# Seven products of block sums for two of eight pairs of k tiles in w_up and w_down, w_up as [token, column], operands at another remainder modulo 128

## The chip, the cores and the metric

One Trainium2 chip, of which the kernel uses 1 core in one launch. The metric is the device time of that launch in microseconds (us). Before the change it is 1472.31 us, the median of 3 runs (1471.69, 1472.31 and 1474.75).

## What is computed

One block of a streaming encoder over 256 tokens of width 2048, all in float32: a gated recurrence and a chunked attention, joined by gates, and then a feed-forward layer (MLP) with a squared ReLU. The change touches the MLP and the projection ahead of it; the two branches are left out here.

```python
# x (1, 256, 2048); w_in (2048, 11264); w_out (2048, 2048)
# w_up (2048, 8192); w_down (8192, 2048)
def rms_norm(x, w):
    return x * lax.rsqrt(jnp.mean(x * x, axis=-1, keepdims=True) + EPS) * w

def mixer_block(u, ...):
    z = u @ w_in
    ...
    merged = gate_a * (y_a @ w_branch_a) + gate_b * (y_b @ w_branch_b)
    return merged @ w_out

h = x + mixer_block(rms_norm(x, norm_mix_w), ...)
u = rms_norm(h, norm_mlp_w)
h = h + jnp.square(jax.nn.relu(u @ w_up)) @ w_down
return rms_norm(h, norm_final_w)
```

## The kernel before

**Precision.** Every large product runs on TensorE (PE) in the type fp32r. To keep the accuracy of float32 each operand is held as two fp32r tiles, hi (the value cast to fp32r) and lo (value minus hi). A product is then three: hi by hi, hi by lo, lo by hi, all added into one PSUM bank. `split` makes the two tiles: a cast on ACT (line 87) and a subtraction on DVE (line 88).

**Weights.** `weights` (lines 107 to 144) streams a weight matrix: one 1 MB DMA on SP's queue fills a `raw` tile (3 buffers), and two splits of 1024 columns each make pairs of tiles `wh` and `wl` (4 buffers each, all in the pool `wpool`, which lives as long as the kernel). Loads and splits run ahead of PE as far as the buffers allow: the scheduler gives splits a high priority, and an engine takes its instructions in order.

**Two forms of product.** `gemm` (lines 149 to 171) holds the activations still (128x128) and moves the weights, 512 columns at a time; it gives [token, column], with a bank for each half of the tokens (NM = 2 halves of 128), 2048 being KD = 16 k tiles of 128. Lines 157 to 159 are its three matmuls. `gemm_t` (lines 173 to 194) holds the weights still and moves the activations; it gives [column, token]. There one matmul of 512 columns (line 186, weight hi by activations hi and lo side by side) and one of 256 (lines 185 and 189, weight lo by activations hi) take the place of three, and `add_parts` adds the two halves up. w_up uses `gemm_t`, which leaves u (the MLP's hidden activations) transposed as w_down needs it. w_out, w_down and the branch products use `gemm`.

**Order.** After the two branches and their gates comes the loop at lines 613 to 621: for each of four column chunks the products w_branch_a (`ba`) and w_branch_b (`bb`), times their gates, summed into `ga`. `turn` transposes a finished chunk (four 128x128 transposes to a group, line 104) and splits it into `act_m`. Then w_out (lines 630 to 646): for each chunk the rows of x are loaded into `h1` on ACT's queue (line 633), the product is added, transposed, scaled by the norm's gain and split into `act_h`. The norm's factor `rstd2` (one for each token) is turned by `rows` into a row over tokens (lines 236 to 245, called at 651), since w_up's output has tokens along the columns. Line 653 loads the final gain `wf`.

The MLP runs in NQ = 4 quarters of 2048 hidden columns (lines 660 to 697). A quarter has 8 calls of `gemm_t` for w_up, each of 256 columns, followed by ReLU, the factor, the square and the split into `act_u`; then 4 calls of `gemm` for w_down, whose result is added to `h1`. In the last quarter the sums of squares and the final norm are taken, and the output is stored; its last chunk keeps 8 k tiles back (`tail=8`), so that the first token half ends earlier.

**PSUM.** Eight banks: `ps_acc` 2 buffers of two banks, `ps_tp` 2, `ps_sm` 2.

## Time and profile before

| | |
|---|---|
| three timed runs | 1471.69, 1472.31, 1474.75 us; median 1472.31 |
| profiled execution, its own time | 1475.12 us |
| its span, first to last instruction | 1473.3 us |
| mean granted PE clock | 0.996 of full |
| read from memory | 269.57 MB, 184 GB/s over the span |

The profiled execution is 0.2% over the median of the runs, and 1.8 us of it lie outside the span. Its stages, by the busy time in each stretch:

```profile
10.00:250.00 240.00, 229.93 (x1206) 197.12 (x1205) 196.16 (x407) 145.61 (x199) 9.61 (x18) 0.99 0.52 181
250.00:470.00 220.00, 218.75 (x1137) 180.98 (x1137) 119.77 (x202) 108.51 (x175) 9.13 (x27) 1.00 0.51 171
470.00:662.00 192.00, 192.00 (x860) 159.18 (x859) 101.16 (x97) 81.53 (x86) 0.00 (x0) 1.00 0.56 190
662.00:757.00 95.00, 95.00 (x442) 78.42 (x441) 57.36 (x63) 44.03 (x58) 0.00 (x0) 1.00 0.61 215
757.00:943.00 186.00, 185.57 (x945) 157.58 (x945) 104.56 (x104) 84.62 (x93) 0.71 (x1) 1.00 0.54 189
```

A row is a stretch (from:to) and its length, then busy us and instructions of PE, PEld (the weight load of a matmul, which overlaps PE), DVE, ACT and POOL, then the granted clock, the share of the DMA engines and GB/s. The first two rows are the input projection with the two branches, the third the gates and the branch products, the fourth w_out, the fifth the first quarter of the MLP. A matmul's busy time counts from its start to its modelled end, and successive ones overlap: the distance from start to start is what one costs. Instruction groups in the profile carry the names of tiles (out<-in) with buffer numbers left out; a line can be that of a helper, so `wl_dn L88` is the subtraction of `split` for a piece of w_down.

### The profile page before, as it was taken

Reading aid. Unit: us, or ns where it says so; the run is one execution under the profiler, and the core shown is the slowest. Engines: PE = TensorE matmul, PEld = TensorE weight load, DVE = VectorE, ACT = ScalarE, POOL = GpSimd, SP = SyncE. Lnnn points to the kernel's source line nnn. Section 1 sums busy time; section 2 is a strip of 40 time slices with the busy share of each in tenths; the row PEclk is TensorE's granted clock in tenths of the full one; section 3 lists DMA queues with packets and bytes.
Section 4 is the critical chain, followed back from the end, with each engine's and each line's share of the span. In section 5 each row is a group of like instructions: output and inputs, shape, how many; then the busy total and the mean of one; then the engine's idle time right before and its main releaser. Section 6 shows DMA issues by size and latency. Waiting matters only on the chain.

```text
span 1473.3 us, 18041 instructions
## 1 busy us (share of the span) xinstructions
PE 1450.8 (98%) x7244; PEld 1222.4 (83%) x7244; DVE 879.8 (60%) x1180; ACT 709.8 (48%) x892; POOL 29.9 (2%) x86
## 2 busy tenths in 40 slices
PE   8999999999999999999999999999999999999997
PEld 7878888888788888888888888888888888888886
DVE  6797977565644444666566655565545665555554
ACT  6754844364544444444445543455344543355443
POOL 2000001010000000000000000000000000000000
PEclk9999999999999999999999999999999999999999
DMA  8644444545455555557545555555555555555552
GB/s 293 223 145 144 170 171 128 198 133 184 134 189 185 194 200 195 180 195 258 197 173 181 192 198 186 188 184 190 198 199 177 197 183 191 198 178 194 199 186 101
DMA packets 48932, 272.85 MB, mean 185 GB/s; under 512 B 5056, under 2 KB 5824, under 8 KB 23376
## 3 DMA queue, kind: packets, MB, share of 16 engines
q1 hardware_dynamic: 45600, 264.78, 51.6%
q10 hardware_dynamic: 2448, 4.74, 0.9%
q0 software_dynamic: 800, 2.16, 0.8%
q8 instruction: 57, 0.93, 0.2%
q14 instruction: 27, 0.22, 0.0%
HBM read 269.57 MB, written 2.10 MB: 184 GB/s over the span
## 4 chain that ended last, share of the span: by engine, by line
PE 92%; DVE 3%; DMA 2%; ACT 1%; issue 1%; POOL 0%; SPq 0%; POOLq 0%; ACTq 0%
PE acc_up L186 16%; PE acc_dn L159 8%; PE acc_dn L158 8%; PE acc_dn L157 8%; PE acc_up L185 8%; PE acc_ak L186 2%; PE acc_wo L157 2%; PE acc_wo L158 2%; PE acc_wo L159 2%; PE acc_gb L158 2%; PE acc_gb L157 2%; PE acc_gb L159 2%; PE acc_ga L159 2%; PE acc_ga L158 2%; PE acc_ga L157 2%; PE acc_aq L186 2%
## 5 line engine op out<-in xcount | busy, mean ns | idle before, releaser
L186 PE MATMUL acc_up<-act_h,wh_up 128*128 128x512 f32 x1024 | 359.3, 398 | 0.0
L185 PE MATMUL acc_up<-act_h,wl_up 128*128 128x256 f32 x960 | 269.8, 281 | 0.0
L88 DVE TENSOR_TENSOR wl_dn<-raw_dn,wh_dn 128x1024 fp32r<-128x1024 f32 x128 | 156.6, 1224 | 149.6 <-ACT wh_dn L87 149.6
L186 PEld LDWEIGHTS acc_up<-act_h,wh_up 128*128 128x128 f32 x1024 | 190.6, 188 | 44.5
L87 ACT CAST wh_dn<-raw_dn 128x1024 fp32r<-128x1024 f32 x128 | 134.9, 1054 | 186.5 <-PE acc_dn L159 172.4
L88 DVE TENSOR_TENSOR wl_up<-raw_up,wh_up 128x1024 fp32r<-128x1024 f32 x128 | 156.5, 1223 | 106.2 <-ACT wh_up L87 106.2
L159 PE MATMUL acc_dn<-wh_dn,act_u 128*128 128x512 f32 x512 | 199.2, 389 | 0.0
L158 PE MATMUL acc_dn<-wl_dn,act_u 128*128 128x512 f32 x512 | 199.2, 389 | 0.0
L157 PE MATMUL acc_dn<-wh_dn,act_u 128*128 128x512 f32 x512 | 199.1, 389 | 0.0
L87 ACT CAST wh_up<-raw_up 128x1024 fp32r<-128x1024 f32 x128 | 134.4, 1050 | 121.4 <-PE acc_up L186 93.4
L185 PEld LDWEIGHTS acc_up<-act_h,wl_up 128*128 128x128 f32 x960 | 181.3, 189 | 1.4
L157 PEld LDWEIGHTS acc_dn<-wh_dn,act_u 128*128 128x128 f32 x512 | 96.1, 188 | 20.1 <-DVE h L678 0.2
L158 PEld LDWEIGHTS acc_dn<-wl_dn,act_u 128*128 128x128 f32 x512 | 96.1, 188 | 20.1
L159 PEld LDWEIGHTS acc_dn<-wh_dn,act_u 128*128 128x128 f32 x512 | 96.1, 188 | 19.6
L88 DVE TENSOR_TENSOR wl_gb<-raw_gb,wh_gb 128x1024 fp32r<-128x1024 f32 x32 | 39.2, 1225 | 47.8 <-ACT wh_gb L87 47.8
L88 DVE TENSOR_TENSOR wl_ga<-raw_ga,wh_ga 128x1024 fp32r<-128x1024 f32 x32 | 39.2, 1225 | 43.4 <-ACT wh_ga L87 43.4
L88 DVE TENSOR_TENSOR wl_wo<-raw_wo,wh_wo 128x1024 fp32r<-128x1024 f32 x32 | 39.2, 1224 | 35.7 <-ACT wh_wo L87 35.7
L87 ACT CAST wh_wo<-raw_wo 128x1024 fp32r<-128x1024 f32 x32 | 33.7, 1054 | 49.4 <-PE acc_wo L159 38.3
L87 ACT CAST wh_gb<-raw_gb 128x1024 fp32r<-128x1024 f32 x32 | 33.8, 1055 | 48.6 <-PE acc_gb L159 42.0
L87 ACT CAST wh_ga<-raw_ga 128x1024 fp32r<-128x1024 f32 x32 | 33.7, 1053 | 45.4 <-PE acc_ga L159 38.6
L186 PE MATMUL acc_hf<-act_x,wh_hf 128*128 128x512 f32 x128 | 48.6, 414 | 3.0 <-DVE f L194 3.0
L159 PE MATMUL acc_ga<-wh_ga,act_x 128*128 128x512 f32 x128 | 50.5, 394 | 0.0
(307 smaller groups left out, 2746.6 us busy)
## 6 DMA issues: line engine op xcount, KB each, us to landing
raw_up<-in_w_up_dram SPq DMA_DIRECT2D x64, 1024.0 KB, 4.9
raw_dn<-in_w_down_dram SPq DMA_DIRECT2D x64, 1024.0 KB, 4.9
raw_ga<-in_w_in_t_dram SPq DMA_DIRECT2D x16, 1024.0 KB, 5.0
raw_gb<-in_w_in_t_dram SPq DMA_DIRECT2D x16, 1024.0 KB, 5.0
raw_wo<-in_w_out_dram SPq DMA_DIRECT2D x16, 1024.0 KB, 4.9
raw_hi<-in_w_in_n_dram SPq DMA_DIRECT2D x8, 1024.0 KB, 4.9
raw_hg<-in_w_in_n_dram SPq DMA_DIRECT2D x8, 1024.0 KB, 4.9
raw_aq<-in_w_in_t_dram SPq DMA_DIRECT2D x8, 1024.0 KB, 4.8
```

What stands on the lines that cost most here:

```text
L87: (copy or nc.scalar.copy)(hi, src)
L88: nc.vector.tensor_tensor(lo, src, hi.bitcast(F32), op=ALU.subtract)
L157: nc.tensor.matmul(part(m), h, wh, start=kt == 0, stop=False)
L158: nc.tensor.matmul(part(m), h, wl, start=False, stop=False)
L159: nc.tensor.matmul(part(m), lo, wh, start=False, stop=kt == nkt - 1)
L185: nc.tensor.matmul(acc[:, cb, 0:T], wl[:, c], r[:, 0, :], start=False, stop=False)
L186: nc.tensor.matmul(acc[:, cb, :], wh[:, c], r.rearrange("p u t -> p (u t)"), start=kt == 0, stop=kt == nkt - 1)
```

## The change

From w_out on the kernel has new helpers; everything ahead of it keeps its code.

- `wpool` and the three PSUM pools are closed after the last branch product. A new pool `spool` holds `raw` tiles of 4 KB a partition (7 buffers), and `wh` and `wl` (6 each); `ps_k` has 7 banks, `ps_tp2` one. `piece` loads two k tiles of 512 columns (512 KB), or one; `parts` splits them.
- `gemm2` is `gemm` with these helpers. It serves w_out and the last two chunks of w_down in the last quarter.
- `gemm_s` computes two chunks of 512 columns at once, for both token halves: 2x2 blocks of the result, as [token, column]. For two pairs of k tiles (0 and 1 with 4 and 5) it takes 7 products in place of 8, by the scheme of Strassen and Winograd: `combos` makes four sums and differences of blocks of the activations once for all calls that share them, four sums of the raw weight pieces are made in place by `add`, and after the seven products five sums (`s1`, X, W, Y, Z) are taken out of the banks into SBUF. The other 12 k tiles go on as before, into four banks that hold, or start from, a part of the seven. At the end each block is bank plus or minus its tile. A call has 186 matmuls of 512 columns, where plain products would have 192.
- w_up goes through `gemm_s` (two calls a quarter), so u has tokens along the partitions: `rstd2` is the scale of a ReLU on ACT, and u is transposed, in 8 groups of four transposes a quarter, between the seven products and the rest of the next call. w_down goes through `gemm_s` too, but for the two chunks named; its result is folded into the tiles with `h1` ahead of the end.
- `mhalf` grows from 4 to 32 columns and `room` of 8 columns is new and not used otherwise: they shift the SBUF addresses of the tiles behind them. Every fp32r operand's address leaves the remainder 32 when divided by 128 before the change, and 0 after it.

```diff
-    wpool = ctx.enter_context(tc.tile_pool(name="wpool", bufs=1))
     apool = ctx.enter_context(tc.tile_pool(name="apool", bufs=8))
     small = ctx.enter_context(tc.tile_pool(name="small", bufs=4))
-    ps_acc = ctx.enter_context(tc.tile_pool(name="ps_acc", bufs=2, space=PSUM))
-    ps_tp = ctx.enter_context(tc.tile_pool(name="ps_tp", bufs=2, space=PSUM))
-    ps_sm = ctx.enter_context(tc.tile_pool(name="ps_sm", bufs=2, space=PSUM))
+    wpool_cm = tc.tile_pool(name="wpool", bufs=1)
+    wpool = wpool_cm.__enter__()
+    ps_cms = [tc.tile_pool(name=n, bufs=2, space=PSUM) for n in ("ps_acc", "ps_tp", "ps_sm")]
+    ps_acc, ps_tp, ps_sm = [cm.__enter__() for cm in ps_cms]
...
-    mhalf = const.tile([P, 4], F32, name="mhalf")
-    nc.gpsimd.memset(mhalf, -0.5)
+    mhalf = const.tile([P, 32], F32, name="mhalf")
+    nc.gpsimd.memset(mhalf[:, 0:4], -0.5)
+    room = small.tile([P, 8], F32, name="room", tag="room", bufs=1)
+    nc.gpsimd.memset(room, 0.0)
...
     turn(3)
     bpool_cm.__exit__(None, None, None)
+    wpool_cm.__exit__(None, None, None)
+    for cm in ps_cms[::-1]:
+        cm.__exit__(None, None, None)
     mp = ctx.enter_context(tc.tile_pool(name="mpool", bufs=1, reuse_waits="tile"))
+    RT, WB, TB = 7, 6, 9
+    sp = ctx.enter_context(tc.tile_pool(name="spool", bufs=1, reuse_waits="tile"))
+    ps_k = ctx.enter_context(tc.tile_pool(name="ps_k", bufs=7, space=PSUM, reuse_waits="tile"))
+    ps_tp = ctx.enter_context(tc.tile_pool(name="ps_tp2", bufs=1, space=PSUM, reuse_waits="tile"))
...
+    def piece(w, n0, kt, q, what):
+        raw = sp.tile([P, 2 * NC], F32, name=f"raw_{what}", tag="rt", bufs=RT)
+        if w.shape[-1] < NC:
+            nb = NC // T
+            src = w[n0 // T:n0 // T + nb, kt // 8, :, kt % 8:kt % 8 + q, :].rearrange("c p a n -> p c a n")
+            nc.sync.dma_start(raw[:, :q * NC].rearrange("p (c a n) -> p c a n", c=nb, n=T), src)
+        else:
+            nc.sync.dma_start(raw[:, :q * NC].rearrange("p (a n) -> p a n", n=NC), w[n0 // NC, kt // 4, :, kt % 4:kt % 4 + q, :])
+        return raw[:, :q * NC]
+    def parts(raw, w, q, what):
+        made = [sp.tile([P, 2 * NC], F32R, name=f"{n}_{what}", tag=n, bufs=WB)[:, :q * NC] for n in ("wh", "wl")]
+        dst, src = made, raw
+        if w.shape[-1] < NC:
+            dst = [t.rearrange("p (a c n) -> p a c n", a=q, n=T) for t in made]
+            src = raw.rearrange("p (c a n) -> p a c n", a=q, n=T)
+        with tc.high_priority(offset=2000):
+            split(dst[0], dst[1], src)
+        return [t.rearrange("p (a n) -> p a n", a=q) for t in made]
+    def bank(what):
+        return ps_k.tile([P, NC], F32, name=f"acc_{what}", tag="k")
+    def mm3(acc, hi, lo, wh, wl, first, last):
+        nc.tensor.matmul(acc, hi, wh, start=first, stop=False)
+        nc.tensor.matmul(acc, hi, wl, start=False, stop=False)
+        nc.tensor.matmul(acc, lo, wh, start=False, stop=last)
...
+    def gemm2(lhs, w, n0, what, kt0=0, tail=0):
+        acc = [bank(f"{what}{m}") for m in range(NM)]
...
+        for k in range(0, KD, 2):
+            ps = (k, *parts(piece(w, n0, kt0 + k, 2, f"{what}{k}"), w, 2, f"{what}{k}"))
+            if k >= KD - tail:
+                held.append(ps)
+                continue
+            for m in range(NM):
+                mm(m, *ps)
...
+    def combos(lhs, n, what):
+        full = []
+        for j in range(2):
+            f = mp.tile([P, n, T], F32, name=f"full_{what}{j}", tag="tmp", bufs=TB)
+            nc.vector.tensor_tensor(f, lhs[j][:, :n, 0, :].bitcast(F32), lhs[j][:, :n, 1, :].bitcast(F32), op=ALU.add)
+            full.append(f)
+        a11, a21 = full[0][:, :, :P], full[0][:, :, P:]
+        a12, a22 = full[1][:, :, :P], full[1][:, :, P:]
+        made = {}
+        s = {i: mp.tile([P, n, P], F32, name=f"s{i}_{what}", tag="tmp", bufs=TB) for i in (5, 2, 4, 7)}
+        nc.vector.tensor_tensor(s[5], a22, a21, op=ALU.subtract)
+        nc.vector.scalar_tensor_tensor(s[2], s[5], -1.0, a11, op0=ALU.mult, op1=ALU.subtract)
+        nc.vector.tensor_tensor(s[4], a12, s[2], op=ALU.add)
+        nc.vector.tensor_tensor(s[7], a11, a21, op=ALU.subtract)
+        for i in (5, 7, 2, 4):
+            t = mp.tile([P, n, 2, P], F32R, name=f"S{i}_{what}", tag=f"S{i}{what[0]}", bufs=1)
+            split(t[:, :, 0, :], t[:, :, 1, :], s[i])
...
+    def gemm_s(lhs, S, w, n0, groups, what, kt0=0, between=None, fold=None):
+        n1 = n0 + NC
+        b = {i: bank(f"{what}p{i}") for i in ("1", "5", "7", "6", "11", "12", "21")}
+        j = 0
+        nS = sum(groups)
+        for q in groups:
+            B = {}
+            for i, (n, k) in {"22": (n1, 4 + j), "12": (n1, j), "11": (n0, j), "21": (n0, 4 + j)}.items():
+                B[i] = piece(w, n, kt0 + k, q, f"{what}{i}_{j}")
+            def add(dst, a, c):
+                with tc.high_priority(offset=2000):
+                    nc.vector.tensor_tensor(B[dst], B[a], B[c], op=ALU.add)
+            def product(i, lh, src, n):
+                wh, wl = parts(B[src], w, q, f"{what}{n}_{j}")
+                for a in range(q):
+                    mm3(b[i], *lh(j + a), wh[:, a], wl[:, a], j + a == 0, i in "1567" and j + a == nS - 1)
+            def of(m, jj):
+                return lambda k: lhs_of(lhs, k + 4 * jj, m)
+            def comb(i):
+                return lambda k: [S[i][:, k, u, :] for u in range(2)]
+            product("1", of(0, 0), "11", "p1")
+            product("12", comb(4), "22", "p3")
+            add("22", "12", "22")
+            add("12", "11", "12")
+            product("5", comb(5), "12", "p5")
+            product("7", comb(7), "22", "p7")
+            add("11", "22", "11")
+            product("6", comb(2), "11", "p6")
+            product("11", of(0, 1), "21", "p2")
+            add("21", "11", "21")
+            product("21", of(1, 1), "21", "p4")
+            j += q
+        tmp = lambda n: mp.tile([P, NC], F32, name=f"{n}_{what}", tag="tmp", bufs=TB)
+        s1, X, W, Y, Z = (tmp(n) for n in ("s1", "sx", "sw", "sy", "sz"))
+        nc.scalar.copy(s1, b["1"])
+        nc.vector.tensor_tensor(X, b["6"], s1, op=ALU.add)
+        nc.vector.tensor_tensor(W, b["5"], X, op=ALU.add)
+        nc.vector.tensor_tensor(Y, b["7"], X, op=ALU.add)
+        nc.vector.tensor_tensor(Z, b["7"], W, op=ALU.add)
+        if fold:
+            for m, n, t, op in ((0, 0, s1, ALU.add), (1, 0, Y, ALU.add), (0, 1, W, ALU.subtract), (1, 1, Z, ALU.subtract)):
+                nc.vector.tensor_tensor(t, t, fold(m, n), op=op)
+        if between:
+            between()
+        b["22"] = bank(f"{what}p8")
+        rest = []
+        for k, stop in ((nS, 4), (4 + nS, KD)):
+            while k < stop:
+                q = 1 if k % 2 else 2
+                rest.append((k, q))
+                k += q
+        for k, q in rest:
+            end = k + q == KD
+            for n in range(2):
+                wh, wl = parts(piece(w, n0 + n * NC, kt0 + k, q, f"{what}r{n}_{k}"), w, q, f"{what}r{n}_{k}")
+                for m in range(NM):
+                    i = "12"[m] + "12"[n]
+                    for a in range(q):
+                        mm3(b[i], *lhs_of(lhs, k + a, m), wh[:, a], wl[:, a], i == "22" and (k, a) == (nS, 0), end and a == q - 1)
+        return [(0, 0, b["11"], s1, ALU.add), (1, 0, b["21"], Y, ALU.add), (0, 1, b["12"], W, ALU.subtract), (1, 1, b["22"], Z, ALU.subtract)]
+    groups, dgroups = (2,), (2,)
...
-        acc = gemm(mT, w_out, n * NC, KD, f"wo{n}")
+        acc = gemm2(mT, w_out, n * NC, f"wo{n}")
...
+        if n == 1:
+            S = combos(hT, sum(groups), "h")
...
-    rstd2_t = rows(rstd2, "rstd2")
...
+    def down(uT, Su, qd, last):
+        for n0 in (0, 2):
+            if last and n0:
+                for n in (2, 3):
+                    acc = gemm2(uT, w_down, n * NC, f"dn{qd}{n}", kt0=qd * KD, tail=8 if n == 3 else 0)
+                    for m in range(NM):
+                        yield n, m, acc[m], None, None
+                continue
+            for m, n, acc, t, op in gemm_s(uT, Su, w_down, n0 * NC, dgroups, f"dn{qd}{n0}", kt0=qd * KD,
+                                           fold=lambda m, n: h1[n0 + n][m]):
+                yield n0 + n, m, acc, t, op
...
-        for c in range(8):
-            acc = gemm_t(hT, w_up, qd * (FF // NQ) + c * T, KD, f"up{qd}{c}")
-            r = mp.tile([P, 2, T], F32, name=f"r{qd}{c}", tag="tmp", bufs=4)
-            add_parts(r, acc)
-            nc.vector.scalar_tensor_tensor(r, r, 0.0, bc(rstd2_t, 1, 2), op0=ALU.max, op1=ALU.mult)
-            nc.scalar.activation(r, r, AF.Square)
-            if c % 2 == 0:
-                uT.append(new_act(f"u{qd}{c}"))
-            k = slice(2 * (c % 2), 2 * (c % 2) + 2)
-            split(uT[-1][:, k, 0, :], uT[-1][:, k, 1, :], r)
-        for n in range(4):
-            end = last and n == 3
-            acc = gemm(uT, w_down, n * NC, KD, f"dn{qd}{n}", tail=8 if end else 0, kt0=qd * KD)
+        pend = []
+        def turn():
+            c, rs = pend.pop(0)
+            uT.append(new_act(f"u{qd}{c}"))
+            hi, lo = uT[-1][:, :, 0, :], uT[-1][:, :, 1, :]
             for m in range(NM):
-                t = h1[n][m]
-                nc.vector.tensor_tensor(t, acc[m] if end else acc[:, m, :], t, op=ALU.add)
+                tp = transpose4(rs[m], f"u{qd}{c}{m}")
...
+        def turns():
+            while pend:
+                turn()
+            if len(uT) == 2:
+                Su.update(combos(uT, sum(dgroups), f"u{qd}"))
+        for c in range(0, 4, 2):
+            rs = {}
+            for m, n, acc, t, op in gemm_s(hT, S, w_up, qd * (FF // NQ) + c * NC, groups, f"up{qd}{c}",
+                                           between=turns):
+                with tc.high_priority(offset=2000):
+                    nc.vector.tensor_tensor(t, acc, t, op=op)
+                nc.scalar.activation(t, t, AF.Relu, scale=rstd2[:, m:m + 1])
+                nc.scalar.activation(t, t, AF.Square)
+                rs[m, n] = t
+            for n in range(2):
+                pend.append((c + n, [rs[m, n] for m in range(NM)]))
+        turns()
+        if last:
+            wf = apool.tile([P, D], F32, name="wf", tag="act")
...
+        for n, m, acc, t, op in down(uT, Su, qd, last):
+                end = last and n == 3
+                r = h1[n][m]
+                if t is not None:
+                    nc.vector.tensor_tensor(r, acc, t, op=op)
+                else:
+                    nc.vector.tensor_tensor(r, acc, r, op=ALU.add)
+                t = r
                 if not last:
                     continue
```

More of the change, by code (lines that the diff above doesn't have):

```diff
@@ new lines, in bank, with lhs_of, mm @@
+    def bank(what):
[4 more added lines that the diff above has]
+        nc.tensor.matmul(acc, lo, wh, start=False, stop=last)
+    def lhs_of(lhs, kt, m):
+        return [lhs[kt // 4][:, kt % 4, u, m * P:(m + 1) * P] for u in range(2)]
+    def gemm2(lhs, w, n0, what, kt0=0, tail=0):
+        acc = [bank(f"{what}{m}") for m in range(NM)]
+        held = []
+        def mm(m, k, wh, wl):
+            for a in range(2):
+                mm3(acc[m], *lhs_of(lhs, k + a, m), wh[:, a], wl[:, a], k + a == 0, k + a == KD - 1)
+        for k in range(0, KD, 2):
[6 more added lines that the diff above has]
+        for m in range(NM):
+            for ps in held:
+                mm(m, *ps)
+        return acc
@@ new lines, in combos @@
+    def combos(lhs, n, what):
[15 more added lines that the diff above has]
+            split(t[:, :, 0, :], t[:, :, 1, :], s[i])
+            made[i] = t
+        return made
@@ L650, in tile_hybrid_block @@
     rsqrt(rstd2, ssum2, D, NM)
-    rstd2_t = rows(rstd2, "rstd2")
-    wf = mp.tile([P, D], F32, name="wf")
-    nc.scalar.dma_start(wf, bass.AP(tensor=norm_final_w.tensor, offset=norm_final_w.offset, ap=[[0, P], [1, D]]))
+    def down(uT, Su, qd, last):
[3 more added lines that the diff above has]
+                    acc = gemm2(uT, w_down, n * NC, f"dn{qd}{n}", kt0=qd * KD, tail=8 if n == 3 else 0)
+                    for m in range(NM):
+                        yield n, m, acc[m], None, None
[3 more added lines that the diff above has]
+                yield n0 + n, m, acc, t, op
     ssq3 = small.tile([P, NM, 4], F32, name="ssq3", tag="ssq3")
@@ L679, in tile_hybrid_block @@
                 if not last:
                     continue
-                junk = mp.tile([P, NC], F32, name=f"ysq_{n}_{m}", tag="tmp", bufs=4)
+                junk = mp.tile([P, NC], F32, name=f"ysq_{n}_{m}", tag="tmp", bufs=TB)
                 nc.scalar.activation(junk, t, AF.Square, accum_out=ssq3[:, m, n:n + 1])
```

9 lines of the change are left out of this document (6 added, 3 removed).

## The prediction

> **What bounds the kernel now.** I read the page first, then the chain of waits, busy times by stage, and the timeline where stages meet.
>
> ```profile
> span 1473.3 us, 18041 instructions
> ...
> PE 1450.8 (98%) x7244; PEld 1222.4 (83%) x7244; DVE 879.8 (60%) x1180; ACT 709.8 (48%) x892; POOL 29.9 (2%) x86
> ...
> PE 92%; DVE 3%; DMA 2%; ACT 1%; issue 1%; POOL 0%; SPq 0%; POOLq 0%; ACTq 0%
> ...
> L186 PE MATMUL acc_up<-act_h,wh_up 128*128 128x512 f32 x1024 | 359.3, 398 | 0.0
> ...
> L88 DVE TENSOR_TENSOR wl_dn<-raw_dn,wh_dn 128x1024 fp32r<-128x1024 f32 x128 | 156.6, 1224 | 149.6 <-ACT wh_dn L87 149.6
> ...
> L87 ACT CAST wh_dn<-raw_dn 128x1024 fp32r<-128x1024 f32 x128 | 134.9, 1054 | 186.5 <-PE acc_dn L159 172.4 <-PE acc_up L186 12.4 <-ACT ysq L682 1.7
> L159 PE MATMUL acc_dn<-wh_dn,act_u 128*128 128x512 f32 x512 | 199.2, 389 | 0.0
> ```
>
> PE is 98% busy and 92% of the chain, and the L186 and L159 rows have no idle before them. ACT and DVE, which split each weight piece, wait for PE to free a buffer (172.4 us on the L87 row). The 398 and 389 ns overlap, so the price of a matmul is the distance of starts. The chain gives it:
>
> ```profile
> 943.09 0.46 PE acc_up L186 x2
> 954.38 0.46 PE acc_up L186 x2
> ...
> 1120.42 0.46 PE acc_up L186 x2
> ```
>
> The pairs mark where one 256-column block of w_up ends and the next begins. A block is 11.29 us: 32 matmuls of 512 columns and 32 of 256. Quarter to quarter is 177.33 us; less eight blocks (90.3) leaves 87.0 for the 384 w_down matmuls, 0.2267 each.
>
> ```profile
> 943.43:1120.77 177.34, 177.34 (x898) 150.56 (x897) 99.07 (x96) 80.48 (x89) 0.00 (x0) 1.00 0.55 190
> ```
>
> That stage (columns: length, then busy us of PE, PEld, DVE, ACT, POOL; clock, DMA share, GB/s) has PE without a gap at full clock, DVE at 56%, DMA at 55%.
>
> **The change, part by part** (minus is faster).
>
> 1. w_up as [token, column]. 512 columns took 2 blocks, 22.57 us; now 16 k tiles x 2 token halves x 3 products = 96 matmuls x 0.2267 = 21.76. Over 16 such chunks: -12.9.
>
> 2. Seven products for eight. Two pairs of k tiles save 6 of 192 matmuls per call of gemm_s. There are 8 calls for w_up and 7 for w_down (the last two column chunks use gemm2): 90 x 0.2267 = -20.4.
>
> 3. New transposes of u: 4 quarters x 4 chunks x 2 halves = 32 groups of four. A group's price:
>
> ```profile
> 685.32 0.39 PE L157 MATMUL acc_wo<-wh_wo,act_m 128*128 128x512 f32 x1
> 685.58 0.66 PE L104 MATMUL tp_h<-ident,h 128*128 128x128 f32 x4
> 685.99 0.48 PE L158 MATMUL acc_wo<-wl_wo,act_m 128*128 128x512 f32 x1
> ```
>
> From L157 to L158 is 0.67 in place of 0.227: 0.44. The group among w_up matmuls at 754.03 costs 0.36. I take 0.43: +13.8 (11.5 to 14.4).
>
> 4. rows(rstd2) goes (its transposes at 758.34 held PE 0.76 us longer than a matmul): -0.8.
>
> 5. The turn into w_out, the main cost. Before, wpool carries on: w_out's first pieces are split while the last w_branch_b product runs, and PE does some 15 w_out matmuls ((665.19 - 661.79) / 0.2267) while DVE finishes the gate:
>
> ```profile
> 661.99 1.29 DVE L617 TENSOR_TENSOR gate_gb<-acc_bb,gate_gb 128x512 f32<-128x512 f32 x2 [0.41 <-PE acc_bb L159]
> ...
> 664.33 1.29 DVE L621 TENSOR_TENSOR gate_ga<-gate_ga,gate_gb 128x512 f32<-128x512 f32 x2
> ```
>
> ```profile
> 665.19 1.19 PE L104 MATMUL tp_m<-ident,gate_ga 128*128 128x128 f32 x8
> ```
>
> ```profile
> 668.52 1.99 ACTq L633 DMA_DIRECT2D h<-in_x_dram  x3
> ```
>
> Now wpool and all PSUM pools are closed and spool starts cold. In the built program PE goes from acc_bb straight to tp_m, then w_out; ACT has act_m's two casts, three loads of h1 and only then the first cast of w_out; DVE likewise puts act_m's two subtractions first. From where PE could go on (661.79 before): gate_gb at 0.20, both done 1.49, first gate_ga 2.17, plus 0.18 (665.19 less 664.33, less 0.68) transposes at 2.35, the second group ends at 3.47; two act_m casts (0.59 each) end at 4.25; three ACT issues at 0.33 to 0.48 end at 5.3 to 5.7; first w_out cast (1.05) at 6.4 to 6.8; PE does two matmuls and waits for the subtraction (1.22) to about 8.0. PE's own work in this is 0.87 + 0.45. Stall: +6.6 (4 if the issues cost ACT nothing and a subtraction slips ahead; 8 if a load is late: raw_wo00 lies where wl_bb3_2 lay, so it can start only some 5.4 us before the w_branch_b product ends, and the 1 MB loads land in 4.9). Its queue, SP, holds nothing else then.
>
> The stall also costs clock:
>
> ```profile
> 30.96 0.39 PE L186 MATMUL acc_hq<-act_x,wh_hq 128*128 128x512 f32 x1
> 34.34 0.67 PE L186 MATMUL acc_hf<-act_x,wh_hf 128*128 128x512 f32 x1 [2.99 <-DVE f L194]
> ```
>
> ```profile
> 34.00:38.00 4.00, 3.65 (x12) 3.17 (x13) 3.16 (x4) 3.50 (x5) 0.00 (x0) 0.57 1.01 426
> ```
>
> After 2.99 us idle the next 4 us had 0.57 of the clock: 4.00 x 0.43 = 1.7 us lost. The new stall holds an idle of about 3 us (3.47 to 6.4): +1.7 (0 to 1.7).
>
> The Trainium skill (TensorE: Matmul & The Clock Gate, Part 1) halves the clock after at least one whole idle window of some 3.4 us; by that this idle is too short and the sum 1.7 lower. The trace disagrees with so late a limit (2.99 us sufficed), so the row stands.
>
> 6. One transpose bank in place of two, and new hand-overs. With every split at WB=6 pairs ahead, I followed one w_up to w_down boundary from the last matmul (0): weight pairs come free at -8.2, -5.4, -2.7 and 0 us; the sixth product's split ends at 2.6 and is due at 7.2, the seventh's at 6.8 and is due at 8.6; relu and square of the first quarter-tile end at -0.9, before its transposes at 0. The second group of u (PE 5.0) finds the bank freed at 5.2, the third waits 0.2. So 0.2 to 0.5 at four boundaries, as much at w_out's transposes: +2 (0 to 8, that is 0.5 at each of 15 calls).
>
> 7. Hidden. Extra splits (19 for 16 per call), four sums of raw pieces, five evacuations and the S tiles raise DVE to about 150 us of a 172 us quarter: per call 23 x 1.22 + 8 x 0.69 = 33.6, 2.8 more for w_down's fold, 2.7 for u's transposes, 4.6 a quarter for S. If that cover went, rival A. Loads become 512 KB in runs of 2 KB (w_up). The page's queues:
>
> ```profile
> q1 hardware_dynamic: 45600, 264.78, 51.6%
> q10 hardware_dynamic: 2448, 4.74, 0.9%
> ```
>
> q1's packets average 5.8 KB and move 21.8 GB/s per engine, q10's average 1.9 KB and move 22: small runs cost no more. A piece needs 1.5 us of 16 engines against 2.72 us of PE work (12 matmuls).
>
> 8. Remainder modulo 128. By the built programs' addresses every fp32r operand, moving and stationary, lies at 32 before and at 0 after: the same remainder within a matmul both times. No row before shows another for fp32r. Bounds: -63 (rival B) to +5 (the 0.236 between starts within w_up's blocks is the slowest steady 512; a tenth of that over 5606 matmuls). I take 0: what is equal stays equal.
>
> The Trainium skill (SBUF — State Buffer, Specifications) gives 16-byte lines, for which 32 and 0 are alike: nothing changes. No trace here has the other value.
>
> Sum: -12.9 - 20.4 + 13.8 - 0.8 + 6.6 + 1.7 + 2 = -10.0, a span of 1463.3. The profiled execution took 1475.12 with its surroundings, 2.8 over the median 1472.31, so the median becomes 1462.3. With all terms at their ends it is 1453 to 1470.
>
> **Rivals.**
>
> A. DVE becomes the bound in the seven products (slower). PE spends 42 x 0.2267 = 9.5 us there; DVE needs 7 splits, 4 sums, 4 evacuations: 16.2 us. For: the gap of 6.7, and DVE is in order. Against: five or six pairs are split ahead while the other 144 matmuls run (32.6 us for 12 splits of 14.7). It decides from 0.7 us of wait per call (10/15). At 2 us per call: 1472.3 - 10 + 30 = 1492.
>
> B. A matmul gets faster at remainder 0. For: fp32 passes, all at 0 or 64, carry almost no surcharge (four tp_m starts 0.109 apart), while 0.2267 is 13 ns over half the 0.42 seen at half clock (34.81 to 35.02 for 256 columns is 0.21). At 0.2154 all 5606 matmuls of 512 save 63: 1399. Against: the surcharge may belong to fp32r, and the transposes mix 64 with 0.
>
> The Trainium skill's back-to-back figure for 512 columns (TensorE: Matmul & The Clock Gate, Back-to-back issue gap) would be this case; the trace's 0.2267 lies above it.
>
> C. The savings are eaten: the turn at 8, hand-overs at 8, transposes at 0.45 leave about -2: 1470. For: part 5 has many steps on one chain. Against: each has a row.
>
> D. It doesn't do what it says: the built program has 186 matmuls per call, so the work is gone; only its time could stay. No chance of its own.
>
> **How the numbers follow.** Forecast 0.64, A 0.13, B 0.13, C 0.10. The likeliest is the sum: 1462, own range 1453 to 1470. To leave out no more than 0.2 the range leaves B out, and half of A: 1450 to 1480. 0.2% (2.9 us) is about what a measurement of this kernel can tell from no change. Faster (below 1469.4): nearly all of the forecast, B, a little of C: 0.78. Same: 0.09. Slower: 0.13.
>
> **What would show it.** w_up and w_down matmuls 0.227 apart, 186 per call; a quarter of 172 to 174 us; one PE gap of 6 to 7 us before w_out with a low clock after it; four tp_u per group at 0.43. Wrong if PE waits for wl tiles of the products (A), if starts lie 0.215 apart (B), or if w_out starts without a gap.

## The result and the profile after

The changed kernel takes 1465.62 us (median of 4 runs, 1465.15 to 1466.51). Runs of the kernel before beside them have a median of 1473.53 (4 runs, 1471.69 to 1475.31). The ratio is 0.9941 with a 95% interval of 0.9922 to 0.996: 7.9 us faster, where 10.0 was forecast, and inside the likeliest case's own range. One run of e9 below (1794.72 us, the clock at 0.75), the only one of e9 with a profile, fell into a slower state of the chip and is left out of e9's time.

The profiled execution after took 1465.54 us. From its page:

```profile
span 1463.7 us, 17979 instructions
...
PE 1438.9 (98%) x6768; PEld 1193.3 (82%) x6768; DVE 1043.8 (71%) x1389; ACT 761.8 (52%) x972; POOL 29.8 (2%) x87
...
PE 86%; DVE 6%; ACT 4%; issue 2%; DMA 1%; POOL 0%; ACTq 0%; POOLq 0%; SPq 0%
...
L664 PE MATMUL acc_wo<-wh_wo,act_m 128*128 128x512 f32 x128 | 51.0, 400 | 2.7 <-ACT wh_wo L90 2.7
```

PE is as busy as before, with 476 instructions fewer. DVE and ACT have come onto the chain (10% in place of 4%), and the w_out row now shows idle time ahead of it, released by the first cast. A quarter of the MLP, by busy times (columns as before):

```profile
934.00:1107.07 173.07, 173.02 (x778) 142.54 (x776) 142.29 (x151) 94.01 (x108) 0.00 (x0) 1.00 0.58 195
```

173.07 us in place of 177.34, PE still without a gap, DVE at 82% in place of 56%.

Starts of matmuls in the two timelines give where the span's 9.6 us came from:

| stretch, us | before | after | difference |
|---|---|---|---|
| to the last w_branch_b matmul | 661.56 | 659.41 | -2.15 |
| from it to the first of w_up (w_out) | 91.42 | 100.34 | +8.92 |
| first quarter | 178.90 | 174.25 | -4.65 |
| second and third quarter, each | 177.33 | 173.07 | -4.26 |
| fourth, to the last matmul | 177.20 | 174.18 | -3.02 |
| from the last matmul to the end | 9.56 | 9.37 | -0.19 |

The first row is taken as no effect of the change: PE's instructions up to there are the same in the same order, and the difference is already 2.16 us after 200 of them, 42 us into the changed kernel, where the execution before had 0.57 of the clock from 34 to 38 us and the one after had all of it. The stretch also varies between executions (657.51 us in e12 and 660.04 in e3 below, which run the same instructions up to there). Without it the change is worth -7.45 us in the spans, which fits the medians.

The turn into w_out in the timeline of the changed kernel (start, duration, engine, line, operation):

```profile
659.41 0.39 PE L162 MATMUL acc_bb<-wh_bb,act_yb 128*128 128x512 f32 x1
659.84 1.29 DVE L620 TENSOR_TENSOR gate_gb<-acc_bb,gate_gb 128x512 f32<-128x512 f32 x2 [8.15 <-PE acc_bb L162]
661.05 1.28 DVE L624 TENSOR_TENSOR gate_ga<-gate_ga,gate_gb 128x512 f32<-128x512 f32 x2
...
661.88 1.94 PE L107 MATMUL tp_m<-ident,gate_ga 128*128 128x128 f32 x8 [2.07 <-DVE gate_ga L624]
663.00 0.59 ACT L90 CAST act_m<-tp_m 128x512 fp32r<-128x512 f32 x1 [12.90 <-PE tp_m L107]
...
663.86 1.30 ACTq L789 DMA_DIRECT2D h<-in_x_dram  x3
...
665.43 1.04 ACT L90 CAST wh_wo<-raw_wo 128x1024 fp32r<-128x1024 f32 x1 [0.99 <-issue]
...
666.51 5.77 DVE L91 TENSOR_TENSOR wl_wo<-raw_wo,wh_wo 128x1024 fp32r<-128x1024 f32 x5 [1.35 <-ACT wh_wo L90]
...
666.53 1.22 PE L664 MATMUL acc_wo<-wh_wo,act_m 128*128 128x512 f32 x2 [2.71 <-ACT wh_wo L90]
```

PE could have gone on at 659.64 and does its first w_out matmul at 666.53. The chain is the one of the prediction: gate operations, transposes, act_m's casts, three load issues, the first cast (ends 6.8 us after 659.64; 6.4 to 6.8 forecast), the subtraction (8.1; 8.0 forecast). The clock:

```profile
658.00:661.90 3.90, 1.83 (x9) 1.20 (x8) 2.06 (x4) 0.00 (x0) 0.00 (x0) 1.00 0.89 289
662.00:672.00 10.00, 7.25 (x20) 5.26 (x21) 7.20 (x8) 6.01 (x7) 0.00 (x0) 0.50 0.92 315
672.10:676.00 3.90, 3.90 (x18) 3.20 (x18) 0.70 (x2) 1.05 (x1) 0.00 (x0) 1.00 0.95 324
```

It is halved for 10.2 us, from the end of the first idle (2.46 us from start to start) on, so that the transposes already run at half speed. Of the turn's 9 us some 6.8 are there when the first product with `wl` starts (667.79, less 0.87 for the transposes and 0.45 for two matmuls), and 2.1 more come by 672.2 from matmuls at half clock.

### The profile page after: what moved, and what is told of

It reads as the page before. It is cut to its first block, busy times and chain, and to the rows that moved or that the text cites. A ratio compares the mean times of both kernels' runs of the same rounds, so it can differ in the third digit from the quotient of the medians.

```text
span 1463.7 us, 17979 instructions
## 1 busy us (share of the span) xinstructions
PE 1438.9 (98%) x6768; PEld 1193.3 (82%) x6768; DVE 1043.8 (71%) x1389; ACT 761.8 (52%) x972; POOL 29.8 (2%) x87
## 3 DMA queue, kind: packets, MB, share of 16 engines
q0 software_dynamic: 800, 2.16, 0.8%
## 4 chain that ended last, share of the span: by engine, by line
PE 86%; DVE 6%; ACT 4%; issue 2%; DMA 1%; POOL 0%; ACTq 0%; POOLq 0%; SPq 0%
PE acc_wo L664 2%; PE acc_wo L665 2%; PE acc_ak L189 2%; PE acc_wo L666 2%; PE acc_gb L162 2%; PE acc_gb L161 2%; PE acc_gb L160 2%; PE acc_ga L162 2%; PE acc_ga L161 2%; PE acc_ga L160 2%; PE acc_aq L189 2%; PE acc_hq L189 2%; PE ps L413 1%; PE acc_hf L189 1%; DMA raw_hf<-in_w_in_t_dram 1%
## 5 line engine op out<-in xcount | busy, mean ns | idle before, releaser
L664 PE MATMUL acc_wo<-wh_wo,act_m 128*128 128x512 f32 x128 | 51.0, 400 | 2.7 <-ACT wh_wo L90 2.7
L666 PE MATMUL acc_wo<-wh_wo,act_m 128*128 128x512 f32 x128 | 51.0, 398 | 0.0
L665 PE MATMUL acc_wo<-wl_wo,act_m 128*128 128x512 f32 x128 | 50.9, 398 | 0.0
L162 PE MATMUL acc_ga<-wh_ga,act_x 128*128 128x512 f32 x128 | 50.5, 394 | 0.0
L160 PE MATMUL acc_ga<-wh_ga,act_x 128*128 128x512 f32 x128 | 50.3, 393 | 0.0
L161 PE MATMUL acc_ga<-wl_ga,act_x 128*128 128x512 f32 x128 | 50.3, 393 | 0.0
L160 PE MATMUL acc_gb<-wh_gb,act_x 128*128 128x512 f32 x128 | 49.8, 389 | 0.0
L161 PE MATMUL acc_gb<-wl_gb,act_x 128*128 128x512 f32 x128 | 49.8, 389 | 0.0
L162 PE MATMUL acc_gb<-wh_gb,act_x 128*128 128x512 f32 x128 | 49.8, 389 | 0.0
L189 PE MATMUL acc_aq<-act_x,wh_aq 128*128 128x512 f32 x128 | 48.0, 408 | 0.0
L189 PE MATMUL acc_hq<-act_x,wh_hq 128*128 128x512 f32 x128 | 46.3, 401 | 0.0
L189 PE MATMUL acc_ak<-act_x,wh_ak 128*128 128x512 f32 x128 | 45.0, 397 | 0.0
L728 DVE TENSOR_TENSOR raw_up<-raw_up,raw_up 128x1024 f32<-128x1024 f32 x32 | 39.2, 1225 | 1.1
```

Of the source, the lines that this page charges most:

```text
L160: nc.tensor.matmul(part(m), h, wh, start=kt == 0, stop=False)
L161: nc.tensor.matmul(part(m), h, wl, start=False, stop=False)
L162: nc.tensor.matmul(part(m), lo, wh, start=False, stop=kt == nkt - 1)
L189: nc.tensor.matmul(acc[:, cb, :], wh[:, c], r.rearrange("p u t -> p (u t)"), start=kt == 0, stop=kt == nkt - 1)
L664: nc.tensor.matmul(acc, hi, wh, start=first, stop=False)
L665: nc.tensor.matmul(acc, hi, wl, start=False, stop=False)
```

## The experiments

All are edits of the changed kernel, timed beside runs of the kernel before on the same chip; a ratio is to that kernel.

### Operands at other remainders

The unused tile is dropped, widened, or the constant is put back to 4 columns:

```diff
-    room = small.tile([P, 8], F32, name="room", tag="room", bufs=1)      # e1: left out
+    room = small.tile([P, 24], F32, name="room", tag="room", bufs=1)     # e8
+    room = small.tile([P, 16], F32, name="room", tag="room", bufs=1)     # e9
-    mhalf = const.tile([P, 32], F32, name="mhalf")
+    mhalf = const.tile([P, 4], F32, name="mhalf")                        # e2
```

> The changed kernel without the unused tile of 8 columns that shifts what lies behind it. The fp32r operands of a matmul now lie at two remainders modulo 128: 4734 of the 6118 matmuls have one operand at 96 and the other at 0, 1024 the reverse, 360 both at 96. Theory (the remainder costs nothing): 512-column starts stay 0.2267 us apart, time 1465.6 us within 3. Rival (unequal remainders slow a matmul, so that the shift is what keeps the kernel fast): starts 0.236 or more apart, at least 5606 x 0.009 = 50 us more, 1515 us or above.

> The changed kernel with the constant at its old 4 columns and the unused tile kept: both fp32r operands of every matmul at remainder 32, as before the change. Theory (the remainder is free): 1465.6 us within 3, starts 0.2267 apart. Rival (remainder 0 buys something that was hidden in the sum): slower by over 3 us, starts above 0.227.

> The changed kernel with the unused tile at 24 columns in place of 8: most matmuls (4734 + 1024 of 6118) have one operand at remainder 64 and the other at 0. Theory (a matmul is slow where its operands' remainders differ at all): about as slow as with 96 and 0, 1490 to 1500 us, starts of 0.232 to 0.235 us in w_up and w_down, 0.2267 where both are at 64. Rival (only an odd multiple of 32 hurts): 1465.6 us within 3.

> The changed kernel with the unused tile at 16 columns: one operand of 4734 + 1024 matmuls at remainder 32, the other at 0. With 96 and 0 the starts in w_up and w_down were 0.232 to 0.235 us apart, with 64 and 0 0.226 to 0.232. Theory (the cost grows with the distance of the remainders, 32 being the shortest): a mean start below 0.2288, 1467 to 1473 us. Rival (the distance counts either way round, so that 32 is as far as 96): 1490 to 1500 us.

| | remainders | time, us | ratio, 95% interval |
|---|---|---|---|
| the change | 0 and 0 | 1465.62 | 0.9941 (0.9922 to 0.996) |
| e2 | 32 and 32 | 1464.56 | 0.9924 (0.9898 to 0.995) |
| e8 | 64 and 0 | 1473.32 | 0.9997 (0.9978 to 1.0015) |
| e9 | 32 and 0 | 1489 to 1495 | 1.0109 (1.0068 to 1.015) |
| e1 | 96 and 0 | 1497.54 | 1.0141 (1.0099 to 1.0182) |

Which remainder it is makes no difference while both are equal (e2, a middle quarter 173.06 us in place of 173.07): rival B is gone. Unequal ones cost: e1's rival held in its direction, not in its size (0.236 between starts and 1515 us or above). Its timeline shows both kinds within one call, since the combined blocks S lie at 96 like the weights, and the plain activations at 0:

```profile
1093.54 0.39 PE L662 MATMUL acc_dn12p<-wh_dn12p,S_u 128*128 128x512 f32 x1
1093.77 0.39 PE L663 MATMUL acc_dn12p<-wl_dn12p,S_u 128*128 128x512 f32 x1
1094.00 0.39 PE L664 MATMUL acc_dn12p<-wh_dn12p,S_u 128*128 128x512 f32 x1
...
1095.14 0.39 PE L663 MATMUL acc_dn12p<-wl_dn12p,act_u 128*128 128x512 f32 x1
1095.37 0.40 PE L664 MATMUL acc_dn12p<-wh_dn12p,act_u 128*128 128x512 f32 x1
1095.61 0.40 PE L662 MATMUL acc_dn12p<-wh_dn12p,act_u 128*128 128x512 f32 x1
```

The starts step by 0.227 with S and by 0.232 to 0.235 with act_u. A call without transposes (186 matmuls) takes 42.16 us in the change, 42.53 in e8 and 43.25 in e1. Neither of e8's theories held: 64 apart costs about a third per matmul of what 96 does (its steps are 0.226, 0.229 and 0.232 in turn). Not all of e1's 32 us are steps of matmuls. In its profile the clock is at half for 20 us of the attention, where it is full in the change (e1, then the change, columns as before):

```profile
389.50:409.80 20.30, 20.30 (x68) 15.42 (x67) 9.07 (x30) 8.08 (x23) 1.54 (x5) 0.50 0.08 14
389.50:409.80 20.30, 20.30 (x119) 16.61 (x118) 13.10 (x39) 11.64 (x30) 1.26 (x5) 1.00 0.23 66
```

PE falls 9.5 us behind the change there, by the starts of the same instructions (0.2 us behind at 387.4 us of the change, 9.7 at 401.4). Why the clock fell isn't shown; the granted clock of e1's four runs (0.986 to 0.991, where the change has 0.992 and 0.993) leaves room for such a stretch in each. That leaves some 22 us for the remainders. In e9 the rival came out about right: its two runs at 0.996 of the clock take 1489 us, 23 more than the change, so 32 apart is about as slow as 96. So the shift gains nothing over the kernel before, but without the unused tile the change would have been slower than it. The Trainium skill (SBUF — State Buffer, Specifications) gives lines of 16 bytes, by which all of these would be alike; these runs show that they are not, and not why.

### The products left out

All pairs of k tiles get eight products: the parts of `gemm_s` from the seven products to the five sums go, four banks take all 16 k tiles, and the calls of `combos` go.

```diff
-        b = {i: bank(f"{what}p{i}") for i in ("1", "5", "7", "6", "11", "12", "21")}
+        b = {i: bank(f"{what}p{i}") for i in ("11", "12", "21", "22")}
...
-    groups, dgroups = (2,), (2,)
+    groups, dgroups = (), ()
```

> The changed kernel with all eight products for every pair of k tiles: no sums of blocks, no five sums at the end of the seven, all 15 calls with 192 matmuls, the rest (w_up as [token, column], transposes of u, new pools) as in the change. Theory (a matmul left out saves its 0.2267 us, and the extra DVE work is hidden): +90 x 0.2267 = +20.4 us, less up to 2 us of waits of the transposes for a bank, so 1484 to 1487 us. Rival (part of the saving is lost to waits for DVE in the seven products): less than +16 us, below 1482.

1483.42 us, ratio 1.006 (1.004 to 1.008): 17.8 us above the change, 18.5 by the spans (1482.2 and 1463.7), a little under the theory's 1484 us and above the rival's 1482. A call without transposes takes 43.52 us, which is 1.36 = 6 x 0.2267 more than 42.16; times 15 that is 20.4. Most of the missing 1.9 is in the calls with transposes, which exceed 192 x 0.2267 by 2.33 and 1.68 us, against 2.50 and 1.92 over 186 x 0.2267 in the change. So nearly all of the saving arrives. Without it the other parts together make the kernel 9 us slower than before.

### How much cover DVE has left

The sums of raw pieces go to POOL (e4); two groups of seven products instead of one in w_up (e6), and in w_down as well (e7); two groups in w_up with half of the plain pieces' subtractions on POOL (e11, on top of e5 and e10 below).

```diff
-                    nc.vector.tensor_tensor(B[dst], B[a], B[c], op=ALU.add)
+                    nc.gpsimd.tensor_tensor(B[dst], B[a], B[c], op=ALU.add)     # e4
...
-    groups, dgroups = (2,), (2,)
+    groups, dgroups = (2, 2), (2,)                                              # e6, e11
+    groups, dgroups = (2, 2), (2, 2)                                            # e7
...
-        nc.vector.tensor_tensor(lo, src, hi.bitcast(F32), op=ALU.subtract)
+        return a, (eng or nc.vector).tensor_tensor(lo, src, hi.bitcast(F32), op=ALU.subtract)   # e11
```

> The changed kernel with the four sums of raw weight pieces per call on POOL instead of DVE. Theory (DVE is not on the path, so relieving it gains nothing): no gain, 1465.6 us within 3, or slower if a sum takes POOL so long that the seven products wait for it (each product is due 2.72 us after the one before; from 3 us per sum PE would wait). Rival (DVE holds PE up in the seven products): faster by 2 us or more.

1525.24 us, ratio 1.0328 (1.0287 to 1.0369). From its groups:

```profile
L728 POOL TENSOR_TENSOR raw_up<-raw_up,raw_up 128x1024 f32<-128x1024 f32 x32 | 76.8, 2401 | 614.8 <-DVE wl_up00p L91 360.7 <-DVE wl_up02p L91 37.5 <-DVE wl_up12p L91 37.2
```

A sum takes 2.40 us, under the 3 us from which waits were expected, and still each call loses 2.6 to 5.4 us. The expectation looked at one sum. Three follow each other (7.3 us) and hold up the casts behind them, and PE then waits for the last of a call's seven products, whose piece is the fourth sum: in one call that sum ends at 1004.83, and PE waits 1.9 us for the piece's cast and 0.8 for its subtraction. Once a quarter the transposes of u wait 3.5 us for ACT as well. No gain from relieving DVE shows, but the run can't tell that from the chain it made longer.

> The changed kernel with seven products for four of the eight pairs of k tiles in w_up (groups of two, one after the other), w_down as it is; one raw buffer less (6) makes the room. Theory (DVE, 82% busy in a quarter, has cover left): 8 calls x 6 x 0.2267 = 10.9 us less, less the waits of the second group: DVE needs 22 x 1.22 = 26.9 us for both groups, PE 84 x 0.2267 = 19.0, and some five pairs are split ahead, so 0 to 1 us of waits per call: 1455 to 1463 us. Rival (DVE is at its end; the second group waits): over 1.4 us of waits per call, 1466 us or above.

> As the run with two groups in w_up, but in w_down too, at the price of one more pair of split buffers (5 in place of 6). Theory (the cover of DVE lasts): 15 x 1.36 = 20.4 us less than the change, less 0 to 1 us per call, 1445 to 1460 us. Rival (DVE becomes the bound: about 142 + 4 x 8.5 + sums = 180 us of DVE work against 168 of PE in a quarter): a quarter of 178 us or more, 1480 us or above.

1516.54 us (ratio 1.0281, 1.0232 to 1.033) and 1539.65 (1.0442, 1.0397 to 1.0488): both times are the rivals'. A quarter of e6, and what PE waited for most in its MLP (us in total, times, longest):

```profile
945.99:1131.11 185.12, 174.88 (x766) 141.40 (x764) 157.98 (x165) 99.72 (x114) 0.00 (x0) 0.98 0.55 182
```

```profile
PE tp_u L107 <- DVE act_u L91: 5.5, 4, 1.5
PE acc_dn30p L664 <- ACT S_u L90: 4.8, 1, 4.8
```

12 us more than the change's quarter although 2.7 us of matmuls are gone. DVE is busy 158 of 185 us: not full. PE waits 4.8 us in each quarter for the combined blocks of u, and in this one 4.0 more for weight pieces of w_up's calls and 1.4 for the bank of the transposes; in the long wait the clock falls to half, for 6.7 us. The steps of the combined blocks stand behind pieces of w_down in DVE's queue: the sums that they start from end at 1032.5, their first step comes at 1041.24, and DVE has no idle over 0.3 us between. The buffer that made the room is a rival that no run takes apart: ACT waits 15 us for loads in this quarter (4.2 at the longest), where it waits for none in the change. So two groups are too many with these buffers; whether buffers, order or DVE's load sets the limit stays open.

> The version with the covered turn and the shared banks, with two groups of seven products in w_up, and half of the subtractions of the plain pieces (one of the two column chunks) moved from DVE to POOL, where an operation of 1024 columns took 2.40 us. Theory (two groups failed because DVE had no time left, and it gets about 5 us per call back): the 12 us per quarter that two groups in w_up lost shrink to 3 us or less, 1440 to 1460 us. Rival (what fails is the order of DVE's queue and the chain of the sums, not its load): over 6 us per quarter are still lost, 1475 us or above.

1509.64 us, ratio 1.0237 (1.02 to 1.0274). It stands on e10, which turned out to cost 16.9 us by itself, so 36 us are left for two groups on that base, against 51 on the change (e6). The time is the rival's (1475 or above), but it is no clean test: most of the waits are e10's transposes, it has e6's one raw buffer less, and a subtraction into fp32r took POOL 2.8 to 3.2 us where 2.40 had been reckoned. Whether a relieved DVE could carry two groups stays open.

### The turn into w_out

e5 loads and splits w_out's first four k tiles during the branch products into free gate tiles, so that 24 matmuls can follow at once; it also changes the order of what comes after. e12 has the order alone: loads of the first pieces into space that is free early, act_m's transposes after the third piece, the loads of h1 last.

```diff
+            if what == "ba" and n == 3:                       # e5
+                for k in range(4):
+                    raw, *hl = [bp.tile([P, NC], d, name=f"{i}_pre{k}", tag="gate", bufs=16)
+                                for i, d in (("raw", F32), ("wh", F32R), ("wl", F32R))]
+                    nc.sync.dma_start(raw, w_out[0, 0, :, k, :])
+                    with tc.high_priority(offset=2000):
+                        split(*hl, raw)
+                    first.append(hl)
...
+    for k, (wh, wl) in enumerate(first):                      # e5
+        for m in range(NM):
+            mm3(acc0[m], *lhs_of(mT, k, m), wh, wl, k == 0, False)
...
+            if hook and k in hook:                            # e5 and e12
+                with tc.issue_after(i.ins), tc.issue_after(made_by[0].ins), tc.issue_after(made_by[1].ins):
+                    hook[k]()
...
+    hook={6: lambda: turn(3), 8: lambda: loads((0, 1)), 10: lambda: loads((2, 3))}   # e12: 4 for 6
```

> The changed kernel with the turn into w_out covered: w_out's first four k tiles are loaded and split during the branch products, into gate tiles that are free by then, their 24 matmuls follow the last w_branch_b product at once, the last gate sum goes to a tile outside the pool that is closed, its transposes come after the second later piece, and the loads of h1 come behind the casts of the first pieces. Theory (the stall and the halved clock after it are what the turn costs): the PE gap before w_out vanishes, from the last w_branch_b matmul to the first of w_up 92 us in place of 100.1, time 1465.6 - 8 = 1457 to 1458 us. Rival (the wait is for w_out's loads, and returns at the first piece that is loaded after the switch of pools): at least 4 us of it stay, 1461 us or above.

1456.5 us (1455.58 to 1457.03), ratio 0.9872 (0.9833 to 0.9911): the theory held. From its timeline:

```profile
659.98 0.39 PE L162 MATMUL acc_bb<-wh_bb,act_yb 128*128 128x512 f32 x1
660.21 0.39 PE L649 MATMUL acc_wo<-wh_pre,act_m 128*128 128x512 f32 x1
660.40 1.29 DVE L621 TENSOR_TENSOR gate_gb<-acc_bb,gate_gb 128x512 f32<-128x512 f32 x2 [8.15 <-PE acc_bb L162]
```

No gap, and 91.33 us from the last w_branch_b matmul to the first of w_up, as before the change (91.42). The turn had cost 9.0 us.

> The changed kernel with the order at the turn mended but no piece of w_out split ahead of the switch of pools: the first pieces' loads go to space that is free early, their casts stand ahead of act_m's and of the loads of h1 on ACT, act_m's transposes come after the third piece. DVE still does the four gate operations first. Theory (two things make the stall of 6.9 us: ACT's order, and DVE's gate operations ahead of the first subtraction): the gate operations end 2.4 us after the last w_branch_b product, the first subtraction 1.2 later, so PE waits about 3.5 us in place of 6.9 and the clock is not halved: 1465.6 - 3.4 - 2.5 = 1459 to 1461 us. Rival (the order on ACT is all of it): no gap left, 1457 us.

1461.77 us, ratio 0.993 (0.9903 to 0.9957), and 96.66 us over the same stretch: 3.7 us of the turn won, 5.3 left. In its timeline:

```profile
657.73 0.61 PE L672 MATMUL acc_wo<-wh_wo,act_m 128*128 128x512 f32 x2
657.93 1.29 DVE L620 TENSOR_TENSOR gate_gb<-acc_bb,gate_gb 128x512 f32<-128x512 f32 x2 [8.15 <-PE acc_bb L162]
...
660.34 2.35 DVE L91 TENSOR_TENSOR wl_wo<-raw_wo,wh_wo 128x1024 fp32r<-128x1024 f32 x2
661.61 0.50 PE L673 MATMUL acc_wo<-wl_wo,act_m 128*128 128x512 f32 x1 [3.26 <-DVE wl_wo L91]
```

PE starts w_out at once and then waits for the subtraction, which stands behind DVE's four gate operations, as the theory had it (3.5 us). Its last part was wrong: the idle of 3.26 us (658.35 to 661.61) halved the clock all the same, for 3.4 us from 662.1 on, and the time is just above its 1461.

### Banks for the transposes

On e5: the transposes take any of eight banks of one pool, in place of one bank of their own.

```diff
-    ps_k = ctx.enter_context(tc.tile_pool(name="ps_k", bufs=7, space=PSUM, reuse_waits="tile"))
+    ps_k = ctx.enter_context(tc.tile_pool(name="ps_k", bufs=8, space=PSUM, reuse_waits="tile"))
```

> The version with the covered turn, and the transposes take any of eight banks of one pool in place of one bank of their own. Theory (groups of transposes wait for the one bank: the four groups in w_up's second call cost 2.50 us, those in w_down's first 1.92, where 4 x 0.44 would be 1.76): up to 0.9 us less per quarter, 1453 to 1456 us. Rival (what exceeds 0.44 is not the bank but the change of the operand's type or of the data waited for): 1456.5 us within 2, groups as before.

1473.37 us, ratio 0.9981 (0.9959 to 1.0003): 17 us slower than e5, which neither theory expected. With banks free, the schedule puts the transposes of w_up's last two chunks right behind its last matmul, ahead of w_down:

```profile
1018.52 0.39 PE L652 MATMUL acc_up12p<-wh_up12r,act_h 128*128 128x512 f32 x1
1018.75 0.60 PE L108 MATMUL tp_u<-ident,s_up 128*128 128x128 f32 x4
1019.58 0.66 PE L108 MATMUL tp_u<-ident,sy_up 128*128 128x128 f32 x4 [0.23 <-ACT sy_up L887]
1022.27 0.66 PE L108 MATMUL tp_u<-ident,sw_up 128*128 128x128 f32 x4 [2.04 <-ACT sw_up L887]
```

There they wait for ACT's ReLU and square. The single bank had spread them over the next products. In w_out it is alike: two groups of h's transposes follow each other and wait for DVE, and the stretch from the last w_branch_b matmul to the first of w_up takes 94.71 us in place of 91.33. What a second bank would save with the old order wasn't tried.

## Why the prediction was right, and where it was off

- **Parts 1 and 2, fewer matmuls.** Exact: a call without transposes takes 42.16 us, 186 x 0.2267 = 42.17.
- **Part 3, transposes of u, with the hand-overs of part 6.** The mis-sized term. The calls with transposes exceed 186 x 0.2267 by 2.50 and 1.92 us in a quarter, 4.42 for 8 groups or 0.55 each, 17.7 us in all, where 13.8 and 2 were forecast. A group that waits, and one that doesn't:

```profile
990.13 0.68 DVE L91 TENSOR_TENSOR act_u<-tp_u,act_u 128x512 fp32r<-128x512 f32 x1
990.48 0.39 PE L665 MATMUL acc_up12p<-wl_up12r,act_h 128*128 128x512 f32 x1
990.87 0.66 PE L107 MATMUL tp_u<-ident,sy_up 128*128 128x128 f32 x4
991.28 0.47 PE L666 MATMUL acc_up12p<-wh_up12r,act_h 128*128 128x512 f32 x1
991.59 0.39 PE L664 MATMUL acc_up12p<-wh_up12r,act_h 128*128 128x512 f32 x1
...
995.71 0.39 PE L664 MATMUL acc_up12p<-wh_up12r,act_h 128*128 128x512 f32 x1
995.95 0.60 PE L107 MATMUL tp_u<-ident,sw_up 128*128 128x128 f32 x4
996.30 0.48 PE L665 MATMUL acc_up12p<-wl_up12r,act_h 128*128 128x512 f32 x1
996.61 0.40 PE L666 MATMUL acc_up12p<-wh_up12r,act_h 128*128 128x512 f32 x1
```

From 995.71 to 996.61 two matmuls and the group take 0.90: the group costs 0.45, and several matmuls behind it are 5 to 9 ns slower each, some 0.03 in all. So a group without a wait costs about 0.48 (15.4 us for 32, where part 3 had 13.8 and at most 14.4). The step of the prediction that fell short is its price of a group: it was read up to the start of the matmul behind the transposes, and left out that this one's own step is 0.09 longer (0.31 in place of 0.2267). From 990.48 to 991.59 the group costs 0.66: it starts at 990.87 in place of 990.71, once DVE's subtraction has read the one bank (to 990.81). Three of the eight groups of this quarter cost more than 0.45 (0.66, 0.71 and 0.53), and each starts within 0.15 us of the end of such a subtraction. What is over 0.48 a group makes the other 2.3 us; part 6 had its 2 for them and for w_out, where the groups cost 0.49 to 0.54 and had cost 0.53 to 0.55 before the change.

- **Part 4, rows(rstd2).** The first call of w_up took 1.56 us more than its like before and 1.10 now: 0.46 saved, 0.8 forecast. Both hold two groups of h's transposes besides, so this is a net figure.
- **Part 5, the turn.** 9.0 us by e5, 8.3 forecast (6.6 and 1.7), the stall by the steps that were forecast (6.8, 6.6 forecast). e12 splits it: 3.7 us by the order of ACT's casts, the transposes and the loads, 5.3 by DVE's gate operations with the clock behind them. The clock's share (2.1, 1.7 forecast) came by another idle than the forecast one: it fell at 661.9, after the wait for the gate, and not in the idle ahead of the first cast (3.13 us from start to start, about 3 forecast). That an idle short of a whole window would suffice was right against the rule of the Trainium skill (TensorE: Matmul & The Clock Gate, Part 1), which asks for a whole window of some 3.4 us; in this trace 2.46 us from start to start sufficed.
- **Part 7, hidden work.** DVE is busy 142 us of a quarter (150 forecast), the profile lists no wait of PE in that quarter, and e3 puts what the seven products lose at 1.9 us in all. The cover ends soon: e6, with a second group in w_up and a raw buffer less, loses 12 us a quarter.
- **Part 8, the remainder.** 0, as taken, by e2. The step "what is equal stays equal" was the right one, though no row stood behind it; that unequal ones are dear was not known.
- **The sum.** With the measured terms it is -12.9 - 20.4 + 17.7 - 0.5 + 9.0 = -7.1, against -7.45 in the spans from the turn on.
- **The rivals.** A did not come at one group a call; at two, PE does wait for pieces of the seven products, and which of buffers, order and DVE's load makes it wait is open. B fell, and its 0.2154 stands in no row, before or after. C had the direction right: turn, transposes, hand-overs and part 4 cost 2.9 us more than their terms, where C needed 8.

The version that beats both is e5: 1456.5 us, 1.3% under the kernel before.

## What to carry to other kernels

Price a change of algorithm by the distance between starts of the limiting engine's instructions, and then look for its cost at the seams: here the products saved arrived to within 2 us of 20, while one closing of buffer pools took 9 back. Where a new phase needs new buffers, let its first pieces use space that is already free in the old ones, so that the limiting engine has work while the pools change hands. After any change of pools look at the remainders of the two operands' addresses, for one small tile more or less moved this kernel by about 1.5%, and by 2% with the stretch of half clock seen beside it.

## What the runs showed of the hardware

- Steps of fp32r matmuls of 512 columns depend on how far apart the two operands' addresses lie modulo 128: 0.2267 us when equal (0, 32, 64 and 96 alike), 0.226 to 0.232 at 64 apart, 0.232 to 0.235 at 96; by the time of the whole kernel 32 apart is about as slow as 96.
- The clock can be halved after an idle of 2.46 us between starts (the change), and in e3 an idle of the same length at the same place did not do it, but the next one, of 2.76 us, did: by the granted clock of single microseconds it fell at 665.4 there, at 661.9 in the change. It came back at about 672.1 in both. The halved stretches lasted 10.2 us in the change, 6.8 in e3 and 3.4 in e12.
